# Softmax weights normalized by the matmul that transposes them, and weight loads moved to another queue, in a two-layer trunk

## The chip, the cores and the metric

The kernel runs on one core of a Trainium2 chip. The time is what the device takes for one execution, in microseconds; it was run three times, and the median counts. The engines named below are PE (TensorE, with its weight loads as PEld), DVE (VectorE), ACT (ScalarE), POOL (GpSimd) and SP (SyncE, which only issues transfers here).

## The reference

x is 512 tokens of 1024 features. Two layers each do x += norm(mixer(norm(x))) and x += norm(swiglu(norm(x))). The mixer of layer 0 is attention in a window of 128 with 16 query heads of 64 on 4 key heads, rotary positions and a learned sink per head. The mixer of layer 1 is a gated unit with 128x128 position mixing. The change touches layer 0's attention:

```python
s = jnp.einsum('bnqhgd,bnkhd->bnhgqk', qb, kk).astype(jnp.float32) * scale
s = jnp.where(valid[None, :, None, None], s, -jnp.inf)
m = jnp.maximum(jnp.max(s, axis=-1, keepdims=True), sink)
p = jnp.exp(s - m)
denom = jnp.sum(p, axis=-1, keepdims=True) + jnp.exp(sink - m)
probs = (p / denom).astype(vv.dtype)
o = jnp.einsum('bnhgqk,bnkhd->bnqhgd', probs, vv).reshape(B, S, Q_WIDTH)
return o @ w_o + b_o
```

## The kernel before

Weights come from HBM in chunks `raw` of 128x1024 fp32 (512 KB). ACT rounds each to a high part `wh` (L359), and DVE subtracts to get the low part `wl` (L330); for some chunks (8, 10, 12 to 22) ACT writes the negated high part instead (L351) and POOL issues an accumulating DMA that adds `raw` (L354). Every projection is three products on PE (L274): high by high, high by low and low by high. Chunks 0 and 1 hold the weights of V, 2 to 11 those of K and Q in ten tiles of 128 features (one chunk each), 12 to 19 those of the output projection, and from 20 on those of the first feed-forward.

The attention runs so. The transposed input `xg` is split into `hh` (ACT, L1459) and `hl` (DVE, L1462), and V is projected first: its products of high-order weights need each hh and hl, then come the low-order ones. Then come the ten K and Q tiles. Each is scaled by the row norms `rbc` (DVE, L996), copied with its 32-row quarters swapped by four DMAs of SP (the rotation, L1002), combined with cosine and sine on DVE (L1005, L1007, L1008), and split into high (ACT, L1012) and low (DVE, L1015). When tiles are ready, eight units (two head groups of eight heads, four query blocks) go through `scores` (PE, and DVE with the mask and the running minimum, L1092), `softmax` (exponentials on ACT with sums, L1112; sum and reciprocal of four heads on DVE, L1115, L1116; then the weights multiplied by the reciprocal, three heads of four on DVE, L1121, the fourth on ACT, L1125) and `values`: four transpositions on PE into one PSUM bank (L1158), a copy to SBUF by ACT (L1162), and a product with V (L1150). A unit of the first query block has one key tile, the others two, so there are 14 pairs of unit and key tile, and two groups of transpositions for each.

The output projection runs in two halves (L1264, L1279) between and behind the units. Each finished token tile of 128 rows has its squares summed by ACT (L501) and is multiplied by the norm's gain, on POOL (L635) or DVE (L641) as a table `PLAN` says by stage; DVE then forms the norm from one-element instructions (L507 and on), adds to x (L654), and PE makes the transposed input of the feed-forward, for the first two tokens by a product with a diagonal tile (L589), else by transposition (L591), split by ACT (L604) and DVE (L608).

The order on PE, DVE and ACT is that in which a planner emits the instructions. It is part of the program: generators ("sides") yield the time at which they are due, by assumed durations, and the main thread of projections lets those run that are due by its own clock. Each engine then takes its instructions strictly in this order and waits for semaphores. Weight loads are emitted when a slot of the ring of 19 buffers `w` is free, and up to now all on SP's queue, in the same order as the rotations.

Of the kernel before, what the change touches and what calls it, by code (L numbers as in the profile page):

```python
# [6 lines left out]
F32 = mybir.dt.float32  # L7
# [6 lines left out]
P = 128  # L14
# [21 lines left out]
AJ = sum(SETS)  # L36
BJ = NJ - AJ
NQ = AJ // 4
PLAN = [(10.0, 0.0, 1.2, (), (2,)), (6.0, 0.8, 0.0, (3,), (1, 2)), (2.0, 0.3, 1.2, (2, 3), (2,)), (8.0, 0.8, 1.2, (2, 3), (2,)), (6.0, 0.3, 1.2, (2, 3), (2,)), (5.0, 0.3, 1.6, (2, 3), (2, 3)), (10.0, 0.3, 1.2, (2, 3), (2, 3)), (6.0, 0.3, 1.2, (2, 3), (2,))]
LAT = 0.1  # L40
DLAT = 1.7
X_0 = 4.9
RS = (0.27406385, -4.2420223, 5.2654107, -0.90349173, 1.7067959)
RSD = 1.4
NA = 1
SCALE = ("av", "av", "av", "av")
DIAG = (0, 1)
POOL_LOW = ()
ALT = (1, 2, 3)
WARM = 8.0  # L50
ORDER = ("w", 0, 1, 2, "w", 3)
# [101 lines left out]
def trunk_kernel(ctx, tc, x_t, xt, w, cols, rows, ws_t, consts, out):  # L153
# [33 lines left out]
        return t[:, 0], t[:, 1]  # L187

    def small(n, tag="s"):
        return sp.tile([P, 8], F32, tag=tag, name=nm(tag), bufs=4 if tag in ("s2", "mv") else 2)[:, 0:n]  # L190

    halves = [slice(0, 256), slice(256, 512)]
    cols2 = [slice(0, S), slice(S, D)]
# [99 lines left out]
    def fetch(free=0.0, most=NBLK):  # L293
        while len(raws) < min(NCH, most):
            c = len(raws)
            n = len(STREAM[c][0])
            if raw_used[0] + n > NRAW[stage[0] in (2, 6)] or used[0] + raw_used[0] + n > NW:
                return
            if c == NLATE:
                load_x()  # L300
            if c == NLATE + 1:
                nc.sync.dma_start(c_msk[:, 0:256], consts[:, 1024:1280])
                nc.sync.dma_start(c_msk[:, 256:384], consts[:, 1408:1536])
                nc.sync.dma_start(cs[:], consts[:, 0:1024])
                busy["d"] += 2.5
            tiles = []
            for b in reversed(STREAM[c][0]):
                raw = wp.tile([P, CB * P], F32, tag="w", name=nm("raw"))
                nc.sync.dma_start(raw[:], w[b])
                busy["d"] = max(busy["d"], now[0], free) + 1.46  # L310
                tiles.insert(0, raw)
            raw_used[0] += len(tiles)
            raws[c] = (tiles, busy["d"] + DLAT)
# [657 lines left out]
    def attention(nx_in, g1o, nx_out):  # L971
# [2 lines left out]
        used[0] += 1  # L974
        qk = [gp.tile([P, 8, S], F32R, tag="ga", name=nm("ga")) for _ in range(2)]
        kk = [gp.tile([P, 2, S], F32R, tag="gb", name=nm("gb")) for _ in range(2)]

        ready = {}
        rotated, todo_m = [], list(range(8))
# [81 lines left out]
        def scores(u):  # L1061
# [3 lines left out]
            nk = u.nk = (n + 1) * P - k0  # L1065
            tk = slice(k0, k0 + nk)
            st, es, sm = small(8, "st"), small(8, "es"), small(8, "sm")
            if u.home == "m":
                ms = [mp.tile([P, S], F32, tag="m", name=nm("pm"))[:] for _ in range(4)]
            elif u.home == "rt":  # L1070
                ms = [x for _ in range(2) for x in pair()]
            else:
                t = ptile()
                ms = [t[:, g] for g in range(4)]
# [29 lines left out]
        def softmax(u, g2, st, es, sm, f):  # L1104
            yield f
            jj = slice(4 * g2, 4 * g2 + 4)
            js = range(4 * g2, 4 * g2 + 4)
            p = lambda j: u.pt[j // 2][:, j % 2, 0:u.nk]
            nc.scalar.activation(es[:, jj], es[:, jj], AF.Exp)
            A(4, f)  # L1110
            for j in js:
                nc.scalar.activation(p(j), p(j), AF.Exp, scale=-1.0, bias=st[:, j:j + 1], accum_out=sm[:, j:j + 1])  # L1112
                f = A(u.nk, f, 0.28)
            yield f
            nc.vector.tensor_tensor(sm[:, jj], sm[:, jj], es[:, jj], ALU.add)  # L1115
            nc.vector.reciprocal(sm[:, jj], sm[:, jj])  # L1116
            V(4, f, 0.13)
            V(4, f, 0.15)
            f = busy["v"] + LAT
            for j in js[NA:]:  # L1120
                nc.vector.tensor_scalar(p(j), p(j), sm[:, j:j + 1], None, ALU.mult)  # L1121
                f2 = V(u.nk // 2, f, 0.13)
            yield f
            for j in js[:NA]:
                nc.scalar.activation(p(j), p(j), AF.Copy, scale=sm[:, j:j + 1])  # L1125
                f2 = max(f2, A(u.nk, f, 0.18))
            u.ready.append(f2)

        def values(u):
# [3 lines left out]
            yield max(u.ready)  # L1133
            nkt = u.nk // P
            tq = slice(n * P, (n + 1) * P)
            yield from take("acc")
            po = acc()
            todo = []
# [14 lines left out]
                    give("t")  # L1153

            for z, (i, kt) in enumerate(groups):
                pT = aux()
                for g in range(4):
                    nc.tensor.transpose(pT[:, g * P:(g + 1) * P], u.pt[g][:, i, kt * P:(kt + 1) * P], ident)  # L1158
                    now[0] += 0.11
                yield from take("t")  # L1160
                th = tmp()[:]
# [30 lines left out]
                u.pr, u.n, u.ready, u.done, u.nk = pr, n, [], False, 0  # L1192
                order.append(u)

        nsink = sp.tile([P, 16], F32, tag="nsink", name="nsink", bufs=1)
        nc.vector.tensor_scalar(nsink[:], sink_bc, -1.0, None, ALU.mult)
        V(16, now[0])
        homes = {"p": NP, "m": 4, "rt": 0}

        def home(u):  # L1200
# [11 lines left out]
                return False  # L1212
            return True

        def all_scores():
            for i, u in enumerate(order):
                while not home(u):
                    yield now[0] + 0.2
# [52 lines left out]
        for t in range(NB):  # L1271
# [7 lines left out]
                nc.vector.tensor_tensor(m[t][c][:], ps[:], m[t][c][:], ALU.add)  # L1279
                tok.add(c, ps, V(S, now[0] + 0.2))  # L1280
            hold[0] = now[0] + (NB - 1 - t) * 8 * 0.65
        drop()
        drop_after(toks)


# [331 lines left out]
```

## Time and profile before

| | us |
|---|---|
| median of three runs | 1043.14 (1042.13 to 1044.21) |
| the profiled execution | 1045.45 |
| its span | 1043.6 |
| PE busy | 1025.7 |
| DVE busy | 665.0 |
| ACT busy | 453.5 |
| POOL busy | 29.7 |

The attention lasts until about 180 us of the span; the feed-forwards and the gated unit follow and are not touched. A row of the timeline gives start, duration, engine, line, operation, tiles (out<-in) and shapes; in brackets stands the idle time of the engine before it and what ended it. A row of groups gives the count, the busy time, the mean of one in ns, and the idle time. Busy times of matmuls overlap their neighbours, so the distance of starts tells what one costs.

### The profile page before, as it was taken

The numbers are of one execution on the slowest core, as the hardware profiler recorded it, in microseconds if no ns is written. First come the engines' busy times: TensorE is split into PE (matmuls) and PEld (weight loads), VectorE is DVE, ScalarE is ACT, GpSimd is POOL, SyncE is SP. The second block draws the span as 40 slices with busy tenths as digits, with TensorE's granted clock in tenths as the row PEclk, the third lists the DMA queues.
The fourth block names the chain that finished last, engine by engine and source line by source line (L and its number), as shares of the span: only waits on it lengthen the run. The fifth ranks groups of instructions, "written<-read, shape, count | busy, mean of one in ns | idle before, by whom it ended". The sixth has DMA issues, their size and how long they took to land.

```text
span 1043.6 us, 13499 instructions
## 1 busy us (share of the span) xinstructions
PE 1025.7 (98%) x5137; PEld 852.8 (82%) x5137; DVE 665.0 (64%) x1209; ACT 453.5 (43%) x791; POOL 29.7 (3%) x32
## 2 busy tenths in 40 slices
PE   8989999999999999999999999999999999999997
PEld 7867666998888888888889888899888888888886
DVE  5568877643445667778594967474344656787746
ACT  5339896532234333444265343564223334334421
POOL 0001002000000000000010000110000000000000
PEclk8989999999999999999999999999999999999999
DMA  9446546144435445554243332043444544555302
GB/s 349 116 122 173 145 125 166 39 135 142 150 133 182 161 158 182 194 183 159 93 141 100 103 122 76 26 142 121 142 141 162 197 146 148 195 195 184 126 20 81
DMA packets 42961, 148.11 MB, mean 142 GB/s; under 512 B 5344, under 2 KB 5856, under 8 KB 42896
## 3 DMA queue, kind: packets, MB, share of 16 engines
q1 hardware_dynamic: 40224, 139.28, 39.8%
q0 software_dynamic: 1952, 7.02, 3.7%
q8 instruction: 40, 0.66, 0.3%
q10 hardware_dynamic: 720, 0.94, 0.3%
q14 instruction: 25, 0.20, 0.1%
HBM read 135.69 MB, written 2.10 MB: 132 GB/s over the span
## 4 chain that ended last, share of the span: by engine, by line
PE 94%; DVE 2%; DMA 2%; ACT 1%; SPq 0%; issue 0%; DVEq 0%; ACTq 0%
PE acc L274 91%; PE acc L1150 1%; PE aux L1158 1%; DMA rt<-rt 1%; PE aux L591 1%; DMA xg<-xt 1%; SPq L1002 0%; ACT pm L1112 0%; DVE vy L480 0%; DVE x L654 0%; DVE hl L608 0%; DVE rt L1005 0%; DVE rt L1008 0%; DVE rt L1007 0%; DVE rt L996 0%
## 5 line engine op out<-in xcount | busy, mean ns | idle before, releaser
L274 PE MATMUL acc<-hh,wh 128*128 128x512 f32 (+1 forms) x960 | 353.2, 368 | 0.0
L274 PE MATMUL acc<-hl,wh 128*128 128x512 f32 (+1 forms) x960 | 350.9, 366 | 2.1 <-DVE hl L608 2.1
L274 PE MATMUL acc<-hh,wl 128*128 128x512 f32 (+1 forms) x960 | 350.6, 365 | 0.0
L330 DVE TENSOR_TENSOR wl<-raw,wh 128x1024 fp32r<-128x1024 f32 x187 | 227.9, 1227 | 147.3 <-ACT wh L359 76.6
L274 PEld LDWEIGHTS acc<-hl,wh 128*128 128x128 f32 x960 | 181.7, 189 | 31.5 <-DVE hl L608 2.6
L359 ACT ACTIVATE wh<-raw 128x1024 fp32r<-128x1024 f32 x160 | 165.8, 1053 | 92.2 <-PE acc L274 57.6
L274 PEld LDWEIGHTS acc<-hh,wh 128*128 128x128 f32 x960 | 181.7, 189 | 29.5 <-issue 0.2
L274 PEld LDWEIGHTS acc<-hh,wl 128*128 128x128 f32 x960 | 181.6, 189 | 28.9
L274 PE MATMUL acc<-wh,rt 128*128 128x512 f32 x496 | 162.2, 389 | 0.0
L274 PE MATMUL acc<-wh,ga 128*128 128x512 f32 (+1 forms) x344 | 119.9, 396 | 0.0
L274 PEld LDWEIGHTS acc<-wh,rt 128*128 128x128 f32 x496 | 93.1, 188 | 19.3
L274 PE MATMUL acc<-wl,rt 128*128 128x512 f32 x248 | 96.5, 389 | 0.0
L890 DVE TENSOR_TENSOR m<-m,acc 128x512 f32<-128x512 f32 x80 | 51.9, 685 | 44.2 <-PE acc L274 32.9
L274 PEld LDWEIGHTS acc<-wh,ga 128*128 128x128 f32 x344 | 64.4, 188 | 18.5 <-issue 4.1
L274 PE MATMUL acc<-wl,ga 128*128 128x512 f32 (+1 forms) x206 | 79.1, 384 | 0.0
L337 ACT ACTIVATE wh<-raw 128x1024 fp32r<-128x1024 f32 x40 | 42.4, 1059 | 71.9 <-DVE raw L342 69.2
L868 ACT ACTIVATE rt<-t 128x512 fp32r<-128x512 f32 x40 | 25.4, 634 | 87.6 <-DVE t L863 69.2
L274 PEld LDWEIGHTS acc<-wl,rt 128*128 128x128 f32 x248 | 46.6, 188 | 9.7
L342 DVE TENSOR_TENSOR raw<-raw,raw 128x1024 f32<-128x1024 f32 x40 | 48.7, 1219 | 0.0
L777 ACT ACTIVATE t<-acc 128x512 f32<-128x512 f32 (+1 forms) x38 | 20.2, 531 | 59.3 <-PE acc L274 59.3
L274 PEld LDWEIGHTS acc<-wl,ga 128*128 128x128 f32 x206 | 38.8, 189 | 6.2
L635 POOL TENSOR_TENSOR m<-m,row 128x512 f32<-128x512 f32 x12 | 16.8, 1434 | 846.6 <-ACT acc L501 846.6
(150 smaller groups left out, 967.8 us busy)
## 6 DMA issues: line engine op xcount, KB each, us to landing
raw<-w SPq DMA_DIRECT2D x240, 512.0 KB, 3.6
wl<-raw POOLq DMA_DIRECT2D x13, 512.0 KB, 5.0
row<-rows SPq DMA_DIRECT2D x8, 512.0 KB, 4.8
rt<-rt SPq DMA_DIRECT2D x40, 64.0 KB, 2.1
xg<-xt SPq DMA_DIRECT2D x4, 512.0 KB, 8.0
x<-x_t SPq DMA_DIRECT2D x4, 512.0 KB, 11.0
out<-x SPq DMA_DIRECT2D x4, 256.0 KB, 2.1
out<-x ACTq DMA_DIRECT2D x3, 256.0 KB, 2.1
```

What stands on the lines that cost most here:

```text
L274: nc.tensor.matmul(ps, a, b, start=start, stop=stop)
L330: nc.vector.tensor_tensor(wl[:], raw[:], wh[:].bitcast(F32), ALU.subtract)
L337: nc.scalar.activation(wh[:], raw[:], AF.Copy)
L342: nc.vector.tensor_tensor(raw[:], raw[:], tiles[1][:], op)
L359: nc.scalar.activation(wh[:], raw[:], AF.Copy)
L591: nc.tensor.transpose(dst, self.src[t][k // 4][:, (k % 4) * P:(k % 4 + 1) * P], ident)
L635: nc.gpsimd.tensor_tensor(self.m[c][:], self.m[c][:], self.g1[:, cols2[c]], ALU.mult)
L777: nc.scalar.activation(t1[:, hf], pg[:, hf], AF.Silu)
L868: nc.scalar.activation(hi, src, AF.Copy)
L890: nc.vector.tensor_tensor(d, d, ps[i][:], ALU.subtract if sign == "-" else ALU.add)
L1150: nc.tensor.matmul(po[i * 64:i * 64 + 64, :], vt[n - nkt + 1 + kt][:, o:o + 64], todo[2 * kt + i], start=kt == 0, stop=kt == nkt - 1)
L1158: nc.tensor.transpose(pT[:, g * P:(g + 1) * P], u.pt[g][:, i, kt * P:(kt + 1) * P], ident)
```

## The change

The weights p stay as exponentials. In `values`, DVE first builds, for a unit, two tiles of four diagonal 128x128 blocks: the identity times 1/sum of each of four heads, both operands broadcast. The transposition becomes an ordinary fp32 matmul of p (stationary) with the diagonal block (moving), which transposes and scales. One buffer of the ring holds both tiles for all units until the attention ends. The multiplications on DVE and ACT go. The planner's clock still advances by 0.11 for each such matmul.

Beside this: the loads of chunks 5 to 15 are issued by POOL instead of SP; in the stage of the output projection no gain is multiplied by POOL, and DVE may defer those of tokens 2 and 3; the negated sinks `nsink` are made when scores begin rather than before the projections; `sm` has four buffers instead of two.

```diff
-PLAN = [..., (6.0, 0.8, 0.0, (3,), (1, 2)), ...]
+PLAN = [..., (6.0, 0.8, 0.0, (2, 3), ()), ...]
-NA = 1
+POOL_LOAD = range(5, 16)
...
-        return sp.tile([P, 8], F32, tag=tag, name=nm(tag), bufs=4 if tag in ("s2", "mv") else 2)[:, 0:n]
+        return sp.tile([P, 8], F32, tag=tag, name=nm(tag), bufs=4 if tag in ("s2", "mv", "sm") else 2)[:, 0:n]
...
-                nc.sync.dma_start(raw[:], w[b])
+                (nc.gpsimd if c in POOL_LOAD else nc.sync).dma_start(raw[:], w[b])
...
-            f = busy["v"] + LAT
-            for j in js[NA:]:
-                nc.vector.tensor_scalar(p(j), p(j), sm[:, j:j + 1], None, ALU.mult)
-                f2 = V(u.nk // 2, f, 0.13)
-            yield f
-            for j in js[:NA]:
-                nc.scalar.activation(p(j), p(j), AF.Copy, scale=sm[:, j:j + 1])
-                f2 = max(f2, A(u.nk, f, 0.18))
+            f2 = busy["v"] + LAT
             u.ready.append(f2)
...
+            while not dgs:
+                if used[0] + raw_used[0] < NW:
+                    used[0] += 1
+                    dg2 = wp.tile([P, 2, 4, P], F32, tag="w", name=nm("dgn"))
+                    dgs.extend(dg2[:, i] for i in range(2))
+                else:
+                    yield now[0] + 0.2
+            fd = []
+            for i in range(2):
+                nc.vector.tensor_tensor(dgs[i], ident.unsqueeze(1).to_broadcast([P, 4, P]),
+                                        u.sm[:, i:8:2].unsqueeze(2).to_broadcast([P, 4, P]), ALU.mult)
+                fd.append(V(S, now[0]))
+            yield fd[0]
             yield from take("acc")
...
+                if fd[i] > now[0]:
+                    yield fd[i]
                 pT = aux()
                 for g in range(4):
-                    nc.tensor.transpose(pT[:, g * P:(g + 1) * P], u.pt[g][:, i, kt * P:(kt + 1) * P], ident)
+                    nc.tensor.matmul(pT[:, g * P:(g + 1) * P], u.pt[g][:, i, kt * P:(kt + 1) * P], dgs[i][:, g],
+                                     start=True, stop=True)
                     now[0] += 0.11
...
-        nc.vector.tensor_scalar(nsink[:], sink_bc, -1.0, None, ALU.mult)
-        V(16, now[0])
...
         def all_scores():
+            nc.vector.tensor_scalar(nsink[:], sink_bc, -1.0, None, ALU.mult)
+            V(16, now[0])
...
-        drop()
+        drop(2)
         drop_after(toks)
```

On SP, behind the constants of the start, the queue was this (`raw` are weight loads, `rt` rotations of one tile, four DMAs each):

```order
L304 DMA cs_95<-consts 128x1024
L309 DMA raw_40_291<-w 128x1024
L309 DMA raw_62_379<-w 128x1024
L309 DMA raw_68_410<-w 128x1024
L309 DMA raw_71_433<-w 128x1024
L1002 DMA rt_66_404<-rt_66_404 32x512 x4
L1002 DMA rt_74_447<-rt_74_447 32x512 x4
L309 DMA raw_76_464<-w 128x1024
L309 DMA raw_79_484<-w 128x1024
L309 DMA raw_84_533<-w 128x1024
L1002 DMA rt_80_495<-rt_80_495 32x512 x4
L309 DMA raw_89_544<-w 128x1024
```

With the change SP has only one load before the rotations, and POOL has the others, with its accumulating DMAs (`wl`) among them; SP first, then POOL:

```order
L304 DMA cs_95<-consts 128x1024
L309 DMA raw_40_290<-w 128x1024
L1003 DMA rt_66_404<-rt_66_404 32x512 x4
L1003 DMA rt_74_447<-rt_74_447 32x512 x4
L1003 DMA rt_80_495<-rt_80_495 32x512 x4
```

```order
L1482 MEMSET ones_142 128x128
L309 DMA raw_62_379<-w 128x1024
L309 DMA raw_68_410<-w 128x1024
L309 DMA raw_71_433<-w 128x1024
L309 DMA raw_76_464<-w 128x1024
L309 DMA raw_79_484<-w 128x1024
L309 DMA raw_84_533<-w 128x1024
L354 DMA wl_83_511<-raw_76_464 128x1024
L309 DMA raw_89_544<-w 128x1024
```

The loads no longer stand behind rotations; those of POOL stand in turn with its accumulating DMAs.

At the start of the program DVE's queue was this, `nsink` ahead of the first split of weights:

```order
L439 MEMSET first_101 128x8
L1196 TENSOR_SCALAR nsink_121<-c_row_94 128x16
L330 TENSOR_TENSOR wl_31_172<-raw_1_106,wh_30_171 128x1024
L1462 SCALAR_TENSOR_TENSOR hl_20_135<-xg0_96,c_cols_91,hh_12_127 128x512
L1462 SCALAR_TENSOR_TENSOR hl_21_136<-xg0_96,c_cols_91,hh_13_128 128x512
```

With the change it is this:

```order
L439 MEMSET first_101 128x8
L330 TENSOR_TENSOR wl_31_171<-raw_1_106,wh_30_170 128x1024
L1474 SCALAR_TENSOR_TENSOR hl_20_134<-xg0_96,c_cols_91,hh_12_126 128x512
L1474 SCALAR_TENSOR_TENSOR hl_21_135<-xg0_96,c_cols_91,hh_13_127 128x512
L1474 SCALAR_TENSOR_TENSOR hl_22_136<-xg1_97,c_cols_91,hh_14_128 128x512
```

`nsink` moved behind the sums of squares of x, sixteen rows later.

At the end of the attention POOL multiplied the gains of tokens 1 and 2 (L635), between its last accumulating DMAs:

```order
L354 DMA wl_286_1762<-raw_252_1612 128x1024
L635 ISA
L635 TENSOR_TENSOR m_185_1213<-m_185_1213,row_254_1617 128x512
L635 TENSOR_TENSOR m_212_1360<-m_212_1360,row_254_1617 128x512
L354 DMA wl_298_1824<-raw_273_1719 128x1024
L635 TENSOR_TENSOR m_216_1401<-m_216_1401,row_254_1617 128x512
L635 TENSOR_TENSOR m_231_1470<-m_231_1470,row_254_1617 128x512
```

With the change DVE has them (L641), between the additions of projections (L1291) and of x (L654), and the split of a weight chunk follows:

```order
L654 SCALAR_TENSOR_TENSOR x1_88<-m_185_1185,rc_309_1808,x1_88 128x512
L654 SCALAR_TENSOR_TENSOR x1_88<-m_212_1320,rc_309_1808,x1_88 128x512
L1291 TENSOR_TENSOR m_231_1457<-acc_302_1797,m_231_1457 128x512
L641 TENSOR_TENSOR m_216_1367<-m_216_1367,row_258_1588 128x512
L641 TENSOR_TENSOR m_231_1457<-m_231_1457,row_258_1588 128x512
L330 TENSOR_TENSOR wl_314_1843<-raw_288_1734,wh_313_1842 128x1024
L1291 TENSOR_TENSOR m_244_1514<-acc_312_1834,m_244_1514 128x512
L542 SCALAR_TENSOR_TENSOR u_317_1863<-s2_296_1754 128x2
```

Token 1's two stand ten rows higher; all four are ahead of the norm of the first two tokens (L542).

More of the change, by code (lines that the diff above doesn't have):

```diff
@@ L38 @@
 NQ = AJ // 4
-PLAN = [(10.0, 0.0, 1.2, (), (2,)), (6.0, 0.8, 0.0, (3,), (1, 2)), (2.0, 0.3, 1.2, (2, 3), (2,)), (8.0, 0.8, 1.2, (2, 3), (2,)), (6.0, 0.3, 1.2, (2, 3), (2,)), (5.0, 0.3, 1.6, (2, 3), (2, 3)), (10.0, 0.3, 1.2, (2, 3), (2, 3)), (6.0, 0.3, 1.2, (2, 3), (2,))]
+PLAN = [(10.0, 0.0, 1.2, (), (2,)), (6.0, 0.8, 0.0, (2, 3), ()), (2.0, 0.3, 1.2, (2, 3), (2,)), (8.0, 0.8, 1.2, (2, 3), (2,)), (6.0, 0.3, 1.2, (2, 3), (2,)), (5.0, 0.3, 1.6, (2, 3), (2, 3)), (10.0, 0.3, 1.2, (2, 3), (2, 3)), (6.0, 0.3, 1.2, (2, 3), (2,))]
 LAT = 0.1
@@ L976, in attention @@
         kk = [gp.tile([P, 2, S], F32R, tag="gb", name=nm("gb")) for _ in range(2)]
+        dgs = []
         ready = {}
@@ L1067, in scores @@
             st, es, sm = small(8, "st"), small(8, "es"), small(8, "sm")
+            u.sm = sm
             if u.home == "m":
@@ L1193, in attention @@
                 order.append(u)
-        nsink = sp.tile([P, 16], F32, tag="nsink", name="nsink", bufs=1)
-        nc.vector.tensor_scalar(nsink[:], sink_bc, -1.0, None, ALU.mult)
-        V(16, now[0])
         homes = {"p": NP, "m": 4, "rt": 0}
@@ L1213, in home @@
             return True
+        nsink = sp.tile([P, 16], F32, tag="nsink", name="nsink", bufs=1)
         def all_scores():
+            nc.vector.tensor_scalar(nsink[:], sink_bc, -1.0, None, ALU.mult)
+            V(16, now[0])
             for i, u in enumerate(order):
```

## The prediction

> **What bounds the kernel now.** I read the shares of busy time first, then the stretches of the attention stage, then the waits of TensorE in order of time.
>
> ```profile
> span 1043.6 us, 13499 instructions
> PE 1025.7 (98%) x5137; PEld 852.8 (82%) x5137; DVE 665.0 (64%) x1209; ACT 453.5 (43%) x791; POOL 29.7 (3%) x32
> 64.57:175.74 111.17, 110.90 (x637) 77.77 (x635) 86.92 (x291) 88.37 (x237) 15.66 (x16) 1.00 0.57 144
> 58.15:64.57 6.42, 6.38 (x19) 4.92 (x19) 5.71 (x20) 3.77 (x13) 0.00 (x0) 0.50 0.14 33
> ```
>
> The columns of the last two rows are the stretch, its length, then the busy time of PE, PEld, DVE, ACT and POOL, the granted clock, DMA share and GB/s. TensorE is busy for 98% of the span. All that the change touches lies before 200 us. From 64.57 to 175.74, where scores, softmax, transpositions and values are interleaved with projections, TensorE is busy 110.90 of 111.17 us at full clock, while DVE and ACT each have over 22 us free. So in that stretch an instruction added to PE is paid in full and one taken from DVE or ACT is worth nothing. Before 64.57 TensorE does wait, and there the other edits can earn.
>
> **The transposition, on PE.** 28 groups of four transpositions (14 pairs of unit and key tile, two groups each) become 28 groups of four fp32 products with the diagonal tiles. The nearest row of the same operand kinds, fp32 128x128 against an fp32 diagonal of 128 columns, is L589 of the norm.
>
> ```profile
> L1158 PE MATMUL aux<-c_id,p 128*128 128x128 f32 x80 | 12.4, 278 | 0.3 <-ACT t L1162 0.3
> 82.63 0.60 PE L1158 MATMUL aux<-c_id,p 128*128 128x128 f32 x4
> 82.99 0.48 PE L274 MATMUL acc<-hh,wh 128*128 128x512 f32 x1
> 182.24 1.05 PE L589 MATMUL aux<-rt,x 128*128 128x128 f32 x8
> 183.05 0.36 PE L274 MATMUL acc<-hh,wh 128*128 128x256 f32 x1
> ```
>
> Busy figures overlap, so I go by starts. Four transpositions hold PE for 82.99 - 82.63 = 0.36 us. Four diagonal products appear as eight records (two passes) and hold it for 183.05 - 182.24 = 0.81. That is 0.45 a group, **28 x 0.45 = +12.6 us**. The lower bound, should a pass cost less in a dense stream, is one extra pass hidden behind a weight load, some 10; the upper, with the loads of two passes exposed, some 15. The 0.3 us that L1158 waits for ACT is taken as gone: -0.3. A rule that would make this far dearer is in the Trainium skill, page "TensorE: Matmul & The Clock Gate", section Terms: transpose mode is four times faster for FP32. By it a group would go from 0.36 to 1.44 and the edit would cost 30 us. The L589 rows disagree: the ratio is 0.81 / 0.36 = 2.25.
>
> **What DVE and ACT get for it.**
>
> ```profile
> L1121 DVE TENSOR_SCALAR p<-p,sm 128x256 f32<-128x256 f32 x24 | 7.1, 352 | 0.3
> L1125 ACT ACTIVATE p<-p,sm 128x256 f32<-128x256 f32 x8 | 4.0, 502 | 0.2 <-DVE sm L1116 0.2
> L1008 DVE TENSOR_TENSOR rt<-rt 128x512 f32<-128x512 f32 x10 | 6.9, 692 | 0.3
> ```
>
> DVE loses 48 multiplies of at most 0.35 (under 17 us) and gains 16 builds of a 128x512 diagonal tile, about 0.69 each by L1008 (11.0 us); ACT loses 16 copies of at most 0.50 (under 8 us). Both have free time under a full PE, so I cost it at nothing. No build with a broadcast operand is in the trace; at half or twice 0.69 the change of DVE, -11 or +5, stays inside its 24 us free. The new wait is that both diagonal tiles are one buffer for all eight units: a build stands on DVE until PE has finished the previous unit's products, and behind it are the next unit's score reductions. PE is now later than the planner believes, which still books 0.11 a transposition, so that wait can last, but between two units stand at least a value product and three to nine 512-column products, over 2 us, against 1.4 for two builds. I take 0, with +3 as the upper end of this case.
>
> **The start: nsink leaves the head of DVE's queue.**
>
> ```profile
> 9.43 0.17 DVE L1196 TENSOR_SCALAR nsink<-c_row 128x16 f32<-128x16 f32 x1 [8.41 <-DMA c_row<-rows]
> 9.52 1.23 DVE L330 TENSOR_TENSOR wl<-raw,wh 128x1024 fp32r<-128x1024 f32 x1
> 4.96 1.06 ACT L359 ACTIVATE wh<-raw 128x1024 fp32r<-128x1024 f32 x1 [2.28 <-DMA raw<-w]
> 13.13 1.33 ACT L1459 ACTIVATE hh<-xg,c_cols 128x512 fp32r<-128x512 f32 x2 [0.22 <-DMA xg<-xt]
> 15.77 1.41 DVE L1462 SCALAR_TENSOR_TENSOR hl<-xg,c_cols,hh 128x512 fp32r<-128x512 f32 x2
> 11.46 0.58 PE L274 MATMUL acc<-wh,hl 128*128 128x256 f32 x1 [3.33 <-DVE hl L1462]
> 21.51 4.00 PE L274 MATMUL acc<-wl,hh 128*128 128x256 f32 x32
> 10.00:20.00 10.00, 8.54 (x51) 8.54 (x52) 10.00 (x16) 7.84 (x14) 0.00 (x0) 0.66 1.03 413
> ```
>
> DVE stood 8.41 us for a row of constants that only the scores need; wh had been ready since 6.02. So wl can run at 6.0, the first hl is done by 8.0 instead of 11.4, and PE no longer waits 3.33 us nor, as the 0.66 in the last row shows, runs the next part at a lower clock. What limits it then is the last xg tile: landed 13.13, two copies to 14.46, the last hl at 15.2, eight products of 0.12 (32 in 4.00): the low-order products could start at 16.2, not 21.51. That upper bound is 5.3. Against it, the first chunk moved to POOL's queue has nothing to wait for and now loads beside xg: 0.52 MB at 413 GB/s, 1.3 us on that landing. Behind it the next projection needs later chunks and row sums, pushed back by two more moved loads, so the lower bound is 1. **I take -3.0.**
>
> **The rotation: eleven weight loads leave SP's queue.**
>
> ```profile
> 54.26 0.55 PE L274 MATMUL acc<-gb,ga 64*128 64x128 f32 x6
> 58.15 1.20 PE L274 MATMUL acc<-gb,ga 64*128 64x128 f32 x6 [3.34 <-ACT ga L1012]
> 55.30 0.75 DVE L1005 SCALAR_TENSOR_TENSOR rt<-rt,c_cols,cs 128x512 f32<-128x512 f32 x1 [4.59 <-DMA rt<-rt]
> 39.98 4.04 DMA rt<-rt
> 48.73 6.34 DMA rt<-rt
> 40.66 3.03 SPq L309 DMA_DIRECT2D raw<-w  x3
> 49.42 0.53 SPq L309 DMA_DIRECT2D raw<-w  x1
> 48.21 0.90 POOL L354 DMA_DIRECT2D wl<-raw  x1 [45.40 <-ACT wl L351]
> L1002 SPq DMA_DIRECT2D rt<-rt x4: 577/585/596, 33.9 to 35.8; - x4
> DMA to landing us min/median/max: 2.0/2.0/2.0
> L1002 SPq DMA_DIRECT2D rt<-rt x4: 508/592/1259, 67.7 to 70.2; - x4
> DMA to landing us min/median/max: 2.0/2.4/3.2
> ```
>
> The second half of the first scores waits 3.34 us: ACT for L1008, this for the third rotation, whose last piece took 6.34 us to land, and the second had taken 4.04 and held DVE too. With no load beside it a piece takes 2.0; behind an accumulating DMA alone (issued at 65.6) 3.2 at most. The three loads at 40.66 stood in SP's queue behind rotations; now they wait only for buffers that the V projection (its last products start at 21.51) and a weight split free, and are mostly in before the second rotation. The second rotation gains 2.0 and the third up to 4.3, together more than the 3.34. As PE itself comes 3 us earlier, DVE must too: with the row sums 3 us earlier and both copies at 2 to 3.2, I get the third rotation at 46 to 47 and its q tile at 50, against PE's need at 51. After the wait PE ran 6.42 us at clock 0.50, so half of that is lost as well: 3.3 + 3.2 = **-6.5 us**. The bounds are 0 (the wait stays) and -6.5. What speaks against it is a rule of the Trainium skill, page "DMA: Bandwidth & Descriptors", section "Issuing engines are not separate DMA queues": all issuers end on the same 16 engines, so another queue saves only issue time. The 2.0 against 6.34 shows contention, and no run here shows which issuer matters; it stands behind the first rival.
>
> **The end of attention: gains of tokens 1 and 2 go from POOL to DVE.**
>
> ```profile
> 164.80 2.86 POOL L635 TENSOR_TENSOR m<-m,row 128x512 f32<-128x512 f32 x2
> 165.98 1.71 DVE L507 SCALAR_TENSOR_TENSOR u<-sq 128x1 f32<-128x1 f32 x1 [1.27 <-ACT acc L501]
> 174.01 1.23 DVE L480 TENSOR_SCALAR vy<-u 128x2 int32<-128x2 int32 x1
> 178.39 0.15 DVE L507 SCALAR_TENSOR_TENSOR u<-sq 128x1 f32<-128x1 f32 x1
> 184.82 0.69 DVE L641 TENSOR_TENSOR m<-m,row 128x512 f32<-128x512 f32 x1 [0.95 <-ACT acc L501]
> 176.65 1.13 PE L589 MATMUL aux<-rt,x 128*128 128x128 f32 x8 [0.90 <-issue]
> 189.29 0.39 PE L274 MATMUL acc<-hl,wh 128*128 128x256 f32 x1 [1.40 <-DVE hl L608]
> ```
>
> One-element DVE instructions last 1.71 and 1.23 us while POOL multiplies, against 0.15 without it (178.39); that goes. In its place come four DVE multiplies of 0.69 (2.8 us), and in the new order eight diagonal products follow the last projection at once, and a weight split stands ahead of the last hl. PE's waits here, 0.90 and 1.40, could vanish (-2.3) or double (+2.3). Counting DVE's queue from the last token of the first pair, the diagonal comes some 0.9 late, the first hl 1.8 and the last 1.8, about 4.5 in place of 3: **+1.0** after rounding down. The diagonal buffer's place in the ring costs nothing: loads are ahead of PE by then.
>
> **Sum.** 12.6 - 0.3 - 3.0 - 6.5 + 1.0 = +3.8. Against the profiled execution, 1045.45 around a span of 1043.6, that is 1049.2; the median of the runs is 2.3 lower, 1043.14, so **1046.9**. The case's own range, with the unknowns combined, is 1044 to 1050.
>
> **Rivals.**
> (a) The rotation stays late, since loads and copies still meet in the DMA engines: +3.8 + 6.5 = 10.3, 1053.4. For it: the accumulating DMA and a load still come next to the third rotation. Against it: both now stand in POOL's one queue, and 3.2 beside the accumulation alone.
> (b) Builds wait for PE and PE for builds: eight units at 1.4 each, +11 on top at most, about 1055. For it: one buffer; against it: 2 us of PE work between units.
> (c) Faster: the attention stage is paced by the softmax chain through ACT, and PE's 110.90 hides waiting, since ends of matmuls are modelled. Place: 80 to 150 us; price: one us back for each hidden. It decides from 3.8 + 2.1 = 5.9 hidden; with 8, 1038.9. For it: ACT's 88.37; against it: the only wait by L1158 is 0.3.
> (d) The front returns its whole bound (5.3) and the end is clean (-2.3): 12.6 - 0.3 - 5.3 - 6.5 - 2.3 = -1.8, or half of both, about 1043.
> (e) By the page's factor of four, +30 - 8.8: about 1064.
>
> **How the numbers follow.** What a measurement here can tell is 0.2%, 2.1 us. Forecast 0.48 (0.36 slower, 0.12 within), (a) 0.15, (b) 0.07, (e) 0.02: slower; (c) 0.12: faster; (d) 0.16: 0.12 within, 0.04 faster. Together faster 0.16, same 0.24, slower 0.60. The range for 8 in 10 runs from 1040.5, between (c) and (d), to 1053, almost at (a).
>
> **What would show it.** L1168 with two records per product and 0.81 from a group to the next product; no wait of PE before 16 us and none at the first scores, with the clock at 1.00 after them; rotations landing in 2 to 3.2; the stretch from the first full-speed projection to the last value product longer by 12 to 13 us; DVE's one-element instructions at 0.15 beside a larger wait for hl at the end. Wrong it is if groups stay near 0.36, or if PE shows new waits for dgn.

## The result, and the profile after

The changed kernel takes 1057.95 us (median of 4 runs, 1057.52 to 1058.55) against 1043.45 for the kernel before on the same chip: a ratio of 1.0138, interval [1.0126, 1.0151]. It is 14.5 us slower. The forecast was 1046.9 with a range to 1053, so the time lies above the range. In number it is nearest to rival (b), about 1055, whose waits between builds and products did not come; the mechanism that did come, a rotation that stays late, is that of rival (a), 1053.4.

The first rows of the page after:

```profile
span 1055.7 us, 13690 instructions
PE 1036.6 (98%) x5249; PEld 864.7 (82%) x5249; DVE 660.9 (63%) x1181; ACT 449.1 (43%) x775; POOL 30.4 (3%) x39
```

and its waits of PE by engine and line (us in total, times, longest):

```profile
PE acc L274 <- ACT ga L1013: 3.9, 1, 3.9
PE acc L274 <- DVE hl L608: 2.9, 2, 1.6
PE acc L274 <- ACT wh L359: 2.3, 1, 2.3
PE aux L589 <- DVE rt L551: 1.5, 1, 1.5
```

PE is busy for 10.9 us more, DVE and ACT together for 8.5 less: work has gone to the engine that bounds the kernel. The wait for ACT at the first scores (L1012 before, L1013 now) is still there, and longer.

The timeline of PE after: the first K/Q product (25.35 before), the first scores, and a transposition by the diagonal tile with its neighbours.

```profile
22.08 0.40 PE L274 MATMUL acc<-hh,wh 128*128 128x512 f32 x1
...
56.05 1.20 PE L274 MATMUL acc<-gb,ga 64*128 64x128 f32 x6 [3.90 <-ACT ga L1013]
...
81.08 1.16 PE L1168 MATMUL aux<-dgn,p 128*128 128x128 f32 x8
82.00 0.48 PE L274 MATMUL acc<-hh,wh 128*128 128x512 f32 x1
...
82.78 1.06 PE L1168 MATMUL aux<-dgn,p 128*128 128x128 f32 x8
83.59 0.48 PE L274 MATMUL acc<-hh,wh 128*128 128x512 f32 x1
```

Against this profile the start has gained 3.3 us, though PE now waits 2.3 there for the high part of a weight chunk (L359), where the prediction said no wait before 16 us. A group of four products now shows eight records and holds PE for 0.81 (82.78 to 83.59), as L589 had promised, or 0.92 where another block stands ahead of it (81.08). And the wait at the first scores has grown from 3.34 to 3.90, with half the clock behind it; the stretches after (from, to, length, then busy times, clock, DMA share, GB/s):

```profile
56.05:61.62 5.57, 5.53 (x17) 4.26 (x18) 4.88 (x16) 2.92 (x11) 0.00 (x0) 0.50 0.41 124
62.10:175.70 113.60, 113.60 (x703) 83.90 (x702) 73.12 (x240) 76.34 (x203) 11.29 (x14) 1.00 0.50 121
```

From 62.1 on PE does not wait at all until the tail, so nothing that DVE and ACT were relieved of comes back.

What holds the first scores is again a rotation. The rows of DVE's timeline that wait for one, and the issues of SP and POOL:

```profile
39.39 0.75 DVE L1006 SCALAR_TENSOR_TENSOR rt<-rt,c_cols,cs 128x512 f32<-128x512 f32 x1 [3.98 <-DMA rt<-rt]
53.20 0.75 DVE L1006 SCALAR_TENSOR_TENSOR rt<-rt,c_cols,cs 128x512 f32<-128x512 f32 x1 [2.32 <-DMA rt<-rt]
32.95 20.93 SPq L1003 DMA_DIRECT2D rt<-rt  x16
48.50 0.90 POOL L354 DMA_DIRECT2D wl<-raw  x1 [13.49 <-ACT wl L351]
49.15 1.34 POOL L309 DMA_DIRECT2D raw<-w  x2
```

The chain of waits goes through both rotations:

```profile
36.75 2.62 DMA rt<-rt
48.90 4.18 DMA rt<-rt
```

Before, DVE waited 4.59 for the third rotation and hardly for the first. Now the first holds it for 3.98 and the third for 2.32. So the wait was moved, not removed. For the first rotation POOL's issues and the landing of its four pieces show how:

```profile
34.48 0.54 POOL L309 DMA_DIRECT2D raw<-w  x1 [4.66 <-DVE wl L330]
L1003 SPq DMA_DIRECT2D rt<-rt x4: 584/588/590, 33.0 to 34.9; - x4
DMA to landing us min/median/max: 2.0/2.0/4.3
```

Before, on SP's one queue, the next load was issued only behind the eight pieces of two rotations (at 40.66), and these four landed in 2.0. Now POOL issues a load between the third piece and the fourth, and the slowest takes 4.3. The experiments ask which part of the change did this, and what the rest cost.

### The profile page after: what moved, and what is told of

It is laid out like the page before. It is cut to its first block, busy times and chain, and to the rows that moved or that the text cites. A ratio compares the mean times of both kernels' runs of the same rounds, so it can differ in the third digit from the quotient of the medians.

```text
span 1055.7 us, 13690 instructions
## 1 busy us (share of the span) xinstructions
PE 1036.6 (98%) x5249; PEld 864.7 (82%) x5249; DVE 660.9 (63%) x1181; ACT 449.1 (43%) x775; POOL 30.4 (3%) x39
## 4 chain that ended last, share of the span: by engine, by line
PE 91%; DMA 3%; DVE 3%; issue 1%; ACT 1%; SPq 0%; DVEq 0%; ACTq 0%
PE acc L274 87%; PE aux L1168 3%; PE acc L1158 1%; DMA raw<-w 1%; DMA x<-x_t 1%; PE aux L591 1%; DMA rt<-rt 1%; SPq L1003 0%; DVE wl L330 0%; DMA c_cols<-cols 0%; DVE x L654 0%; DVE m L1291 0%; DVE rt L1006 0%; ACT wh L359 0%; DVE rt L1008 0%
## 5 line engine op out<-in xcount | busy, mean ns | idle before, releaser
L359 ACT ACTIVATE wh<-raw 128x1024 fp32r<-128x1024 f32 x160 | 165.8, 1052 | 90.4 <-PE acc L274 57.6
L635 POOL TENSOR_TENSOR m<-m,row 128x512 f32<-128x512 f32 x8 | 11.4, 1421 | 848.9 <-ACT acc L501 848.9
```

Of the source, the lines that this page charges most:

```text
L359: nc.scalar.activation(wh[:], raw[:], AF.Copy)
L635: nc.gpsimd.tensor_tensor(self.m[c][:], self.m[c][:], self.g1[:, cols2[c]], ALU.mult)
```

## The parts, one at a time

Four kernels carry one part or leave one out. First, all but the diagonal tiles:

```diff
-                    nc.tensor.matmul(pT[...], u.pt[g][...], dgs[i][:, g], start=True, stop=True)
+                    nc.tensor.transpose(pT[...], u.pt[g][...], ident)
(and the multiplications of p by 1/sum back in softmax, no dgs, drop())
```

> The changed kernel with the normalization put back where it was (softmax multiplied by 1/sum on DVE and ACT, transpositions by identity, no diagonal tiles); nsink's place, the POOL loads and the new gains' order stay. Theory A (the transposition on PE is what made it slow, about 13.3 of +12.1, the rest of the change sums to about -1.3): 1057.9 - 13.3 = 1044.6, so 1043.5 to 1045.5, and four transpositions back at 0.36 us. Theory B (the diagonal tiles cost only their predicted 12.6 or less and the POOL loads or the end of attention cost the rest): 1046 or more. Theory C (PE's order is paced elsewhere and the products hide waits): 1050 or more, with new waits of PE between 64 and 176 us.

Measured: 1046.28, ratio 1.0022 [1.0013, 1.0032], 0.8 above theory A's upper end and in theory B's window. So in the full change the diagonal tiles are worth 11.7, and the rest is not the gain of 1.3 that the two traces suggested but a loss of 2.7. (PE waits 2.5 us in this run for the attention output, L1178, which it does not do in the full change; the run with the new order of the gains alone, below, shows why.) Next, the diagonal tiles alone:

> The kernel before with the normalization inside the transposition as the only edit. Theory A: +13.0 to +13.6 on the kernel before (28 groups at 0.475), about 1056.5, no wait of PE for a diagonal tile, the wait of 3.3 us at the first scores and the half clock behind it as before. Theory B: +12.6 or less. If builds and products waited for each other only when PE comes early (as it does not here), less than in the full change.

Measured: 1058.45 (four runs, 1053.24 to 1060.05), ratio 1.013 [1.0101, 1.0159]: +14.9, which is 1.3 above theory A's upper end. The timeline of PE shows where the surplus begins, at the tail, and the stretch behind it where it lies:

```profile
190.81 2.88 PE L588 MATMUL aux<-rt,x 128*128 128x128 f32 x16 [2.08 <-DVE rt L550]
```

```profile
193.00:198.00 5.00, 4.28 (x21) 3.98 (x20) 3.94 (x8) 2.30 (x8) 0.00 (x0) 0.50 0.17 70
```

A wait of 2.08 us there is followed by five us at clock 0.50. The full change has 1.47 in that place and 1.00 behind it. The four runs scatter by 6.8 us and their mean clock with them (0.991 at 1059.83, the profiled one, 0.996 at 1053.24), so this surplus does not seem to be in every execution. Then the other two parts, nsink's place and the loads on POOL:

> The kernel before with nsink moved out of the head of DVE's queue as the only edit. Theory A (the start's gain is real and is kept to the end): the first K/Q product about 3.3 us earlier than 25.35, -2.5 to -3.3 on the time, 1040.2 to 1041, with the wait at the first scores still 3 to 4 us. Rival D (what the start gains is lost at the first scores, because the third rotation does not come earlier): wait at the first scores up to 6 us and the time within 0.5 of the kernel before. My prediction said -3.0 for this step.

Measured: 1040.46, ratio 0.9966 [0.9954, 0.9978], -3.1, with the wait at the first scores at 3.14 and the first K/Q product at 21.26. The step is right, and rival D falls: the gain is kept to the end.

> The kernel before with the raw loads of chunks 5 to 15 on POOL's queue as the only edit. The prediction's step (loads off SP's queue let the rotations land in 2 to 3.2 us): the wait of 3.34 at the first scores goes, -6.5. Theory A (the rotations meet the loads in the DMA engines whichever queue issues them): wait and half clock stay, rotation pieces of 6 to 7 us, 0 to +1. Rival E (the POOL loads do help, but in the full change PE came 3 us earlier and so still waited): the wait shrinks by 1 to 3 us here, where PE is not earlier, and the time falls by 1 to 5.

Measured: 1044.34, ratio 1.0009 [1.0000, 1.0019], +0.8. PE's row at the first scores:

```profile
56.85 1.20 PE L275 MATMUL acc<-gb,ga 64*128 64x128 f32 x6 [4.62 <-ACT ga L1013]
```

The wait grew from 3.34 to 4.62. Part of that is PE coming earlier here too (its first scores start at 51.68, at 54.26 before), so the wait alone does not decide on rival E; but the second half of the scores starts at 56.85, against 58.15 and, in a second profile of the kernel before, 56.17, and the time did not fall. Theory A holds in time, wait and half clock; the predicted -6.5 and rival E's 1 to 5 us of gain fall. The last part is the order of the gains:

```diff
-(6.0, 0.8, 0.0, (3,), (1, 2))
+(6.0, 0.8, 0.0, (2, 3), ())
```

> The kernel before with the new order of the gains and of the blocks at the end of attention (the second entry of PLAN) as the only edit. Theory A (the new order suits only a kernel whose TensorE is slowed by the diagonal products; without them PE meets two waits for the attention output, 1.3 and 1.2 us at 160 and 170 us in the run without diagonal tiles): +2.5 to +3.5. Rival F (those waits come from the POOL loads, not from the order): within 1 us of the kernel before. My prediction gave this step +1.0 with bounds of 2.3 either way.

Measured: 1046.02, ratio 1.0023 [1.0014, 1.0033], +2.3, just under theory A's window; rival F falls. PE's order is the same as before; on DVE four gain multiplies are added and one weight split moves behind an addition. The rows of DVE and PE in this run:

```profile
163.41 0.69 DVE L641 TENSOR_TENSOR m<-m,row 128x512 f32<-128x512 f32 x1 [4.62 <-ACT acc L501]
164.02 0.68 DVE L1177 TENSOR_TENSOR ga<-acc,ga 128x512 fp32r<-128x512 f32 x1
164.76 0.72 PE L274 MATMUL acc<-wh,ga 128*128 128x512 f32 x2 [1.31 <-DVE ga L1177]
```

The multiply stands in DVE's queue ahead of the low part of the attention output, and waits 4.62 for ACT's squares; the low part could have run, and PE waits 1.31 for it. The same happens at 174.57 with 1.17. In the full change neither wait exists: PE, slowed by the products, comes later. The counterpart is the full change with the old order:

> The changed kernel with the old order of the gains and blocks at the end of attention, all else kept. Theory A (with the diagonal tiles the old order has a 2 us wait for the norm's squares and a stretch at half clock behind it, as the run with the diagonal tiles alone shows near 190 us): 1058.5 to 1061, 1 to 3 us more than the changed kernel. The prediction's +1.0 for the new order would make it 1057.

Measured: 1059.05, ratio 1.0151 [1.0136, 1.0166], +1.1 on the full change, within theory A's window, though the half clock that theory A named did not occur in its profile (clock 1.00 from 185 to 200) and the two intervals overlap. So the same edit costs 2.3 without the diagonal tiles; that it saves about 1 with them is not clear of the noise.

And the full change with the loads back on SP:

```diff
-POOL_LOAD = range(5, 16)
+POOL_LOAD = ()
```

> The changed kernel with all raw loads back on SP's queue; the order on PE, ACT and DVE is unchanged. Theory A (POOL loads cost about 0.8 to 1.5): 1056 to 1057.3, wait at the first scores 3.1 to 3.4. The prediction gave these loads -6.5, so that without them it would be 1064.

Measured: 1054.37, ratio 1.0102 [1.0083, 1.0121]. The loads on POOL cost 3.6 in the full change, more than theory A's 0.8 to 1.5. The wait at the first scores, which theory A put at 3.1 to 3.4, is 2.65. The views of the input tile x, whose squares give the row norms, show how: first with the loads on SP, then in the full change (durations in ns, first and last start).

```profile
L1493 ACT ACTIVATE j<-x x4: 633/634/634, 15.8 to 20.6; 128x512 f32<-128x512 f32 x4
DMA to landing us min/median/max: 10.7/11.4/12.1
```

```profile
L1493 ACT ACTIVATE j<-x x4: 632/633/637, 17.0 to 23.5; 128x512 f32<-128x512 f32 x4
DMA to landing us min/median/max: 12.2/13.8/15.2
```

In SP's one queue the weights stood behind x. In POOL's they do not, and the DMA engines, whose busy share is 1.03 from 10 to 20 us in both runs, serve both at once: a tile of x takes 2.4 us longer to land, the last square starts 2.9 later, and the first rotation is issued at 32.95 instead of 29.42.

Last, what the builds cost; the weights are not normalized in this run:

```diff
-                nc.vector.tensor_tensor(dgs[i], ident..., u.sm[...]..., ALU.mult)
...
-                    nc.tensor.matmul(pT[...], u.pt[g][...], dgs[i][:, g], start=True, stop=True)
+                    nc.tensor.matmul(pT[...], u.pt[g][...], ident, start=True, stop=True)
```

> The changed kernel with the identity tile as the second operand of its products and the sixteen builds of the diagonal tiles left out; the softmax is not normalized in it. The order of everything else is unchanged. Theory A (the cost is two passes on PE, the builds and the wait for them cost nothing): 1057 to 1058, as the changed kernel. Rival M (products wait for the builds or DVE's 11 us of builds delay the scores' reductions): 1 to 4 us less.

Measured: 1057.24, ratio 1.0126 [1.0109, 1.0143], the full change's within the intervals. The group of builds in the full change says why:

```profile
L1140 DVE TENSOR_TENSOR dgn<-c_id,sm 128x512 f32<-128x512 f32 x16 | 10.3, 683 | 1.2 <-PE aux L1168 1.2
```

Sixteen builds of 0.68 lie under a full PE, and DVE waits for the one buffer 1.2 us in all. The builds cost nothing that these runs can tell (0.7 us, within the intervals); what the diagonal tiles cost is the second pass on PE and what follows from it.

## What makes the third rotation late

Two runs on the kernel with nsink moved. In one the planner believes in a longer rotation and puts more of the next projection ahead of the first scores; in the other the third rotation has no accumulating DMA and few loads beside it.

```diff
-ROT = 4.0
+ROT = 8.0
```

> The kernel before with nsink moved, and the planner told that a rotation takes 8 us and not 4, so that the second half of the first scores stands behind 18 products of the next projection and not behind 3. Theory G (the wait is only a matter of PE's order: 15 more products of 0.227, 3.4 us, cover the 3.1 to 3.3 us, and the half clock goes with the wait): no wait over 0.5 at the first scores, clock 1.00 behind them, 1040.5 - 5 to 6.5 = 1034 to 1036. Rival H (the work that is put ahead only moves the wait to the next tile's scores, whose rotations come later too): a wait of 2 to 4 us appears at the second pair, and the time stays within 1 us of 1040.5.

Measured: 1044.71, ratio 1.0018 [1.0005, 1.0031]. The twelve score products ran without a wait (52.85 to 53.66, no idle time in front), and the 145th product of the K/Q tiles came at 55.14, where the kernel with only nsink moved has it at 62.57. But the time is 4.2 above that kernel. The planner shifted everything behind too, and PE's waits then are

```profile
PE acc L274 <- DVE hl L608: 3.2, 2, 2.8
PE aux L1158 <- ACT t L1162: 3.1, 1, 3.1
PE aux L589 <- DVE rt L551: 1.7, 1, 1.7
```

So the wait can be covered, and up to there the gain is at least what theory G says (7.4 us at the 145th product, 0.7 of it from an earlier start; it said 5 to 6.5), but this edit is no clean test of its worth at the end; neither theory foresaw that it would be lost further on, to a wait of 3.1 at 101 us (L1158) and to those of the tail. Rival H falls, since the second pair of scores does not wait.

```diff
-BY_DMA = (8, 10, 12, ...)
+BY_DMA = (10, 12, ...)
...
+            if c >= 12 and turned[0] < 3:
+                return
```

> The kernel before with nsink moved, chunk 8's low part made by DVE in place of the accumulating DMA, and no load from chunk 12 on until three rotations are done: the third rotation then has neither an accumulating DMA nor new loads beside it. Theory A (rotation pieces of 4 to 7 us are contention with loads and accumulation): all pieces of the third rotation land in 2 to 2.5 us, the wait at the first scores falls to 0 to 1 us. Rival I (DVE's queue is what makes it late, and it now has one more split): pieces of 2 us but a wait that stays over 2. The later stages pay for late loads, so the total is not read here, only the part up to 70 us.

Measured: 1044.92 in all. Up to 70 us, which is what counts, DVE's two rows that take up the third and fourth rotation, and the issues of SP and POOL:

```profile
45.94 0.75 DVE L1008 SCALAR_TENSOR_TENSOR rt<-rt,c_cols,cs 128x512 f32<-128x512 f32 x1
52.76 0.75 DVE L1008 SCALAR_TENSOR_TENSOR rt<-rt,c_cols,cs 128x512 f32<-128x512 f32 x1 [2.68 <-DMA rt<-rt]
41.88 2.41 SPq L1005 DMA_DIRECT2D rt<-rt  x4
44.39 0.53 SPq L312 DMA_DIRECT2D raw<-w  x1
45.91 6.70 SPq L1005 DMA_DIRECT2D rt<-rt  x8
46.73 0.90 POOL L357 DMA_DIRECT2D wl<-raw  x1 [43.92 <-ACT wl L354]
```

The third rotation was there in time (pieces of 2.0 to 2.5 us), and the first scores did not wait: theory A holds, rival I falls. A load was issued right behind it, at 44.39, and did it no harm. The fourth, beside the next accumulating DMA, was late. That points at the accumulating DMA rather than at that load. The clean test moves one ACT instruction, the negated copy of chunk 8 for which that DMA waits, and leaves the order of all others on PE, ACT, DVE, POOL and SP as it is:

```diff
-            nc.scalar.activation(wl[:], wh[:]..., AF.Copy, scale=-1.0)
...
-            nc.gpsimd.dma_start(wl[:], raw[:], accum_op=ALU.add)
+            def emit(): (these two)
+            if c in (8,) and not turned[0]: late.append(emit)
...
                 nc.scalar.activation(dst_h[:, hf], t1[:, hf], AF.Copy)
+                if i == 2:
+                    turned[0] = 1
+                    flush()
```

> The kernel before with nsink moved, and one ACT instruction (the negated copy of chunk 8, with the accumulating DMA that waits for it) put behind the copy of the third rotated tile; every other instruction on every engine keeps its place. Theory J (the accumulating DMA of chunk 8 alone makes the third rotation take 6.4 us; the raw load issued at 45.1 does not): third rotation in 2 to 2.5 us, no wait over 0.5 at the first scores (it was 3.14), clock 1.00 behind them, 3.1 + 2 to 3.4 us less: 1034 to 1035.5. Rival K (the raw load beside it is as bad, or the gain is lost again at the next tiles, whose rotation now meets the moved DMA): wait of 1.5 to 3 us there or at the second pair's scores, 1038 to 1041.

Measured: 1034.47 (1034.28 to 1034.65), ratio 0.9909 [0.9894, 0.9924]: 6.0 less than with nsink alone, and the fastest kernel of the study, 0.9% under the kernel before. The chain of waits of the kernel with nsink alone, POOL's issue there, and the stretch behind its first scores:

```profile
42.58 0.51 SPq L1002
44.41 6.37 DMA rt<-rt
```

```profile
43.88 0.90 POOL L354 DMA_DIRECT2D wl<-raw  x1 [41.06 <-ACT wl L351]
```

```profile
53.85:60.69 6.84, 6.75 (x19) 5.20 (x20) 6.14 (x20) 4.20 (x13) 0.00 (x0) 0.51 0.16 38
```

PE's rows at the first scores with the instruction moved, and the same stretch:

```profile
49.64 0.82 PE L274 MATMUL acc<-gb,ga 64*128 64x128 f32 x10
50.75 0.33 PE L274 MATMUL acc<-gb,ga 64*128 64x128 f32 x2 [0.29 <-DVE ga L1034]
```

```profile
53.85:60.69 6.84, 6.84 (x32) 5.65 (x31) 5.45 (x13) 4.14 (x8) 0.87 (x1) 1.00 0.83 200
```

A piece of the rotation took 6.37 us because the accumulating DMA was issued between the pieces. Without it the wait falls from 3.14 to 0.29 and the clock stays at 1.00; the load at the same place is still there. Theory J holds in wait, clock and time, and rival K falls. One number of theory J was missed: the pieces of the third rotation took 2.7 to 4.0 us and not 2 to 2.5, with no accumulating DMA beside them, but behind three loads of SP that took up to 7.6 us to land. So loads slow a rotation too, only less. The same move in the full change:

> The changed kernel with that same move alone. It asks whether the -6.5 of the prediction for a rotation that lands in time was right in size. Theory J: the 3.90 us wait and the half clock (5.5 us, half of it lost) go, 4 to 6.5 us less, 1051.5 to 1054. Rival L (in the changed kernel the loads on POOL's queue delay the rotations too, its second piece of 4.3 us at 35 holds DVE): the wait only shrinks to 1 to 2.5 us and the half clock may stay, 1055 to 1057.

Measured: 1056.54, ratio 1.0118 [1.0102, 1.0135], only 1.4 less, which is rival L in time; the wait is still 2.8, above rival L's 1 to 2.5, since the first rotation now holds DVE for 5.00. With both causes gone, and with the loads of chunks 8 to 15 alone put back on POOL:

> The changed kernel with the raw loads on SP's queue and the negated copy of chunk 8, with its accumulating DMA, behind the third rotated tile. Theory N (the two causes add: loads on POOL's queue make the first rotations late, the accumulating DMA the third): no wait at the first scores, 1054.4 - 6 = 1047.5 to 1049.5. Rival O (with diagonal tiles the stage behind is bounded by something else, so that an earlier start of it is lost): 1051 to 1054.

Measured: 1049.01, ratio 1.0058 [1.0041, 1.0074], no wait at the first scores, as theory N said. But the two gains do not simply add: alone they were 3.6 (the loads) and 1.4 (the accumulating DMA), together they are 8.9, because either cause alone keeps a wait at the first scores and the half clock behind it.

> As the run with the loads on SP and the moved copy, but chunks 8 to 15 loaded by POOL's queue again; chunks 5 to 7 stay on SP. Rival P (only the early loads hurt, by landing beside the tiles that the row sums need, so that the first rotation is issued at 32.7 and not 29.4): first rotation back at 29.4 and within 1 us of the run with all loads on SP. Rival Q (loads on POOL's queue behind an accumulating DMA hurt wherever they stand): wait of 2 to 4 us at the first scores, 1053 to 1056.5.

Measured: 1051.21, ratio 1.0078 [1.0063, 1.0093]. The first rotation is back at 29.4 and the wait at the first scores down to 0.4 and 0.3, but the median piece of a rotation takes 4.0 us instead of 2.1, and the time is 2.2 above the run before it. Each theory has a share: of the 7.5 us between 1056.54 and 1049.01, 5.3 come from the three early loads and 2.2 from the later ones. Last, the kernel before again:

> The kernel before once more, unchanged. If the wait of 3.3 us at the first scores and the half clock behind it belong to every execution, both are there again; the first K/Q product came at 25.35 in the first profile and at 23.97 and 24.39 in the runs whose start is the same code, so 23.5 to 25.5 here, and a time of 1042 to 1045.5.

Measured: 1043.17 with a span of 1041.4, a wait of 2.71 at the first scores, the half clock behind it, and the first K/Q product at 24.00. Both profiles of the kernel have the wait and the half clock. Not every execution need have them: of 24 runs of it on one chip, 23 took 1041.91 to 1045.53 at mean clocks of 0.992 to 0.995, and one took 1037.36 at 0.997, of which no trace was kept. The first profile was of an execution whose start was 1.35 late, and the clock there can account for it. From 10 to 20 us it had 0.66 (a row of the prediction), here

```profile
10.00:20.00 10.00, 8.96 (x62) 8.96 (x63) 10.00 (x18) 7.89 (x15) 0.00 (x0) 0.83 1.03 411
```

which is 1.7 us of PE's work at full clock.

## Why the prediction was wrong, by its steps

**The rotation, -6.5, is the step that failed.** The prediction held that with the loads off SP's queue the rotations would land in 2 to 3.2 us, so that the wait at the first scores and the half clock behind it would go. The wait was 3.90 and the half clock stayed. The loads on POOL are +0.8 alone and +3.6 in the full change, so the step was off by 7 to 10 us, which is the greater part of the 11 between forecast and result. Its size was right for a rotation that lands in time: 6.0 with nsink moved (1040.46 to 1034.47), 5.4 in the full change on SP's queue (1054.37 to 1049.01).

Two things were wrong in the cause. I read the 6.34 of the third rotation, beside an accumulating DMA and a load, as the load's doing, because behind an accumulation alone I had a row with 3.2 at most. But that rotation was issued 2.1 us after its accumulation; where the accumulation comes between the pieces, the last piece takes 6.2 to 6.4 with the loads on SP's queue, and still 4.2 and 4.6 with them on POOL's. With that DMA moved, the wait went from 3.14 to 0.29. And I took loads in another queue as loads out of the way. SP's order had kept them from being issued between the pieces of a rotation or ahead of x; three of those moved now run beside x, which the rotation needs first, and one comes between the pieces of the first rotation. The step also stood at the better of its own bounds, 0 and -6.5, and the move was given no cost in any other place than the start. Rival (a) had this as "loads and copies still meet in the DMA engines", at 0.15. Its 1053.4 falls short of the result, since it too lets the move cost nothing at the rotations. The rule of the Trainium skill that stood behind it (page "DMA: Bandwidth & Descriptors", section "Issuing engines are not separate DMA queues") held here: another issuer did not make the rotations faster. Between 28 and 58 us their median piece takes 2.2 us before, 3.4 with the loads on POOL alone and 3.7 in the full change.

**The transposition, +12.6, was right in kind and somewhat small.** From the start of each group to the next row, the 28 groups hold PE for 11.14 us before and 24.55 after: +13.4, since not all cost the 0.81 of the row that I took (the first group above has 0.92). Another 0.8 lies in a place that a list of waits does not show, because the time counts as busy:

```profile
160.37 1.08 PE L1158 MATMUL acc<-t,vt 128*64 128x512 f32 x4
161.38 1.16 PE L1168 MATMUL aux<-dgn,p 128*128 128x128 f32 x8
162.47 1.89 PE L1158 MATMUL acc<-t,vt 128*64 128x512 f32 x4
164.29 0.94 PE L1168 MATMUL aux<-dgn,p 128*128 128x128 f32 x6
...
162.63 0.60 ACT L1173 ACTIVATE t<-aux 128x512 f32<-128x512 f32 x1 [0.56 <-PE aux L1168]
```

The second four value products hold PE for 1.82 (162.47 to 164.29) where the first four needed 1.01 (160.37 to 161.38), since ACT's copy ends at 163.23. Rival (e), four times, falls by the same rows: a group went from 0.36 to 0.81, a factor of 2.25. Between the best kernel without diagonal tiles and the one with them, all loads on SP and the accumulation moved in both, stand 14.5 us (1034.47 and 1049.01); this includes the other order at the end.

**DVE's and ACT's relief and the builds, 0:** right, by the run with the identity in their place. Rival (b) falls with it: PE's list of waits names no diagonal tile in the full change, and in three other runs a single wait of 0.3 to 0.5. Rival (c) falls too: PE's busy time hid 0.8 more than before, and nothing came back. Rival (d) falls as well, since the rotation gave nothing and the front no more than 3.3 against the 24.00 of the second profile.

**The start, -3.0:** right for nsink (-3.1 alone). In the full change some 1.3 of it went back to the early loads: the first K/Q product comes at 22.08, with all loads on SP at 20.72 (the run with the accumulation moved), where PE has no wait for L359. The forecast had counted 1.3 us for the first of these loads.

**The end of attention, +1.0:** the mechanism named (what stands ahead of what in DVE's queue) is right, and the sign depends on PE: +2.3 alone, the upper bound, and about -1.1 in the full change, which is not clear of the noise. DVE's one-element instructions last 0.15 as foreseen, and the waits for hl at the end are larger, 2.9 in all against 2.1.

**The sum.** By the two first traces the terms are 13.4 + 0.8 - 0.3 - 2.65 (start, counted to the first scores) + 0.2 (rotation) + 1.35 (waits at the tail, 4.34 against 2.99) = 12.8, against 12.1 between the spans; 0.7 I cannot place. The medians are 14.5 apart: the first profile of the kernel before was some 2 above its median, that of the changed kernel was not. Taking those 2.3 off the forecast was therefore right.

## What to carry to other kernels

A transfer moved to another queue keeps its bytes and loses its rank, so ask what it will now pass, and what waits for that. When a small copy is late, name the one neighbour that makes it so, by moving that one alone: here moving a single ACT instruction was worth 6 us, and moving the eleven loads that looked guilty was worth less than nothing. And parts tried alone need not be worth the same in the whole. Here the four alone sum to +14.9 (14.9 - 3.1 + 0.8 + 2.3), close to the whole's 14.5, but that is luck: within the whole the diagonal tiles cost 11.7 and not 14.9, the loads 3.6 and not 0.8, and the order of the gains costs nothing and may save 1, where alone it costs 2.3. What nsink's place is worth there was not tried.

## What the runs showed of the hardware that I had not expected

- A copy of 64 KB from partition to partition in SBUF (one piece of a rotation) takes 2.0 us with nothing beside it, and 4.0 to 6.4 when an accumulating DMA of 512 KB is issued just before it. Plain loads of 512 KB slow it too: the last piece of the second rotation took 4.0 in the kernel before, with three loads issued right behind it, and the first rotation 4.7 to 5.5 beside POOL's loads in the run with chunks 8 to 15 on POOL. One load issued right behind a rotation left its last piece at 2.0.
- Half clock followed a wait of 2.08 us (at the tail of the run with the diagonal tiles alone) and waits of 2.7 to 4.6 (at the first scores), but not every wait of such a length: 2.30 at the start of the full change, and even 3.41 at the start of the run with only the loads on POOL, left the clock at 1.00. Except at the end of the span it lasted 3.41 or 6.83 us in every trace: 6.83 behind the first scores of the kernel with nsink alone (the row of 53.85:60.69 above), 3.41 in the full change with the loads on SP, the row below. So a wait of this length costs nothing, 1.7 or 3.4 us on top of itself; what decides between them these runs do not show.

```profile
53.73:57.14 3.41, 3.41 (x9) 2.67 (x10) 2.96 (x12) 1.59 (x9) 0.00 (x0) 0.50 0.00 0
```

- The time of a start of the same code varied by 1.4 us between executions (first K/Q product at 23.97, 24.00, 24.39 and 25.35), with the half clock in it.
